# Attention's first head pair: raw q, k and bias rows loaded by ScalarE's queue, both heads in a row, k converted first

## The chip, the cores and the metric

The kernel runs on one core of a Trainium2 chip. The metric is the device time of one execution in microseconds. The kernel before takes a median of 1443.23 us over three runs (1440.9 to 1454.74). One profiled execution, from which all rows come, has a span of 1443.3 us from first to last instruction.

## The reference

One transformer block on a sequence of 1024 tokens and width 1024, all in float32. A vector `c` gives shifts, scales and gates; a normed and modulated `x` is projected by `w_in`. Half of the projection feeds eight heads of attention, the other half a gated delta rule. Both results go through `w_out`, and a gated feed-forward follows. The part that the change touches is attention:

```python
q_a, k_a, v_a, q_d, k_d, v_d, z_d, b_d, a_d = jnp.split(proj, split_points, axis=-1)
y_attn = _dilated_attention(q_a..., k_a..., v_a..., rel_bias)
# three branches (window, dilation) = (128, 1), (512, 4), (2048, 16), each:
s = jnp.einsum('bhrnqd,bhrnkd->bhrnqk', qb * dh ** -0.5, kw) + bias
m = jnp.max(s); e = jnp.exp(s - m); o = e @ v / sum(e)
# and the branches are mixed by a softmax over their log-sums
```

The kernel computes the three branches as one: every pair of positions gets one bias value per head, which holds the bucket's bias and the logarithm of the number of branches that see the pair, or minus 1e30 where none does.

## The kernel before

**Numbers.** A float32 operand of a matmul is split in a high part in the format fp32r and a low part (the rest after rounding), and two or three matmuls are summed. A conversion is therefore two instructions: a copy of ScalarE into the high tile, and a subtraction on GpSimd or VectorE for the low tile. In attention each head has 64 rows of q and 64 of k. A raw tile holds these 64 rows twice, in the upper and the lower 64 partitions, so it takes two loads of 64 rows and 256 KB each. `QS` holds q times -0.125, in one half of the partitions the high part and in the other the low part: ScalarE writes all of it (line 1223) and VectorE then overwrites one half with the rest (1224). `KS` is the high part of k (ScalarE, 1228) and `KL` its low part (GpSimd, 1229). A score is the matmul of `QS` with `KS` (1254) plus that with `KL` (1255). VectorE adds the bias from the tile `ng` while it leaves PSUM (1258); `ng` is 512 KB per head, read with a shifted row for each partition (1231). ScalarE takes the exponential (1263), GpSimd scales it (1265), TensorE turns it (1278) and multiplies it with the values `va` (1295).

**Stages.** After the first projections the delta rule runs, and its scan ends at about 477 us of the span. Then attention runs over four pairs of heads with eight query blocks each. `att_load` (1207) fetches a pair. Its data have been written to DRAM long before by `spill` (1071): for the first pair the last such write left at 430 us. Independent projections fill TensorE's gaps all along: `proj_t` (line 593) and `proj_d` (line 570) are generators whose matmuls are interleaved by `ahead`, `turn` and `attend`. Around the start of attention these are the values of the later pairs (`va1`, eight token blocks of 24 matmuls) and then k and q of the second pair (`a4_1`, `a0_1`). A finished block is copied from its PSUM bank by ScalarE (1061, 1070) and written to DRAM. There are two such banks (`gbank`, tag "g"), so a block can start only when the block before the last one has been copied out. The weights for them come in slabs (`wsplit`, 210): a load on SyncE's queue (215), a high part by ScalarE (216) and a low part by GpSimd (217); three raw, five high and five low slabs are in memory at once.

**Order.** A planner orders each engine's instructions: it walks through the program with estimated durations, and issues on each engine the instruction with the best priority among those that are ready in its walk. Priority is the place in the program; whatever stands in `with urgent():` is taken as 6000 places earlier. The order is fixed then: an engine that waits for one instruction holds back all that stands behind it. Before the change every DMA of the kernel is issued by SyncE (SP in the profile). The planner also gives each DMA one of eight completion counters in turn, shared by all queues, and an issue waits until the earlier DMA on its counter has landed. The tiles of attention (pool `pa`) lie in the memory of the delta rule's tiles (pool `pd`), which is closed just ahead; the four raw tiles lie on the tiles `qk` that the last readout of the scan reads (1011), and in the order of before the first load of the new pool stands behind the last write of the scan (1043).

Of the kernel before, what the change touches and what calls it, by code (L numbers as in the profile page):

```python
# [10 lines left out]
F32 = mybir.dt.float32  # L11
F32R = mybir.dt.float32r
AF = mybir.ActivationFunctionType
ALU = mybir.AluOpType
# [4 lines left out]
P = 128  # L19
T = 1024  # L20
# [50 lines left out]
def build(tc, I, out):  # L71
    nc = tc.nc
    es = ExitStack()
    op = es.enter_context

    def pool(name, side="left", bufs=1, space=None):
        st = ExitStack()
        kw = {} if space is None else {"space": space}
        p = st.enter_context(
            tc.tile_pool(name=name, bufs=bufs, side=side, reuse_waits="tile", **kw)  # L80
        )
        return p, st
# [10 lines left out]
    def urgent():  # L93
        return tc.high_priority(offset=6000)
# [10 lines left out]
        out=tri, in_=tri, pattern=[[1, P]], compare_op=ALU.is_ge, fill=0.0,  # L105
# [71 lines left out]
    for j in range(3):  # L177
        n = min(HALF, 1152 - HALF * j)
# [146 lines left out]
    for k in range(KT):  # L325
# [6 lines left out]
        if k == 0:  # L332
            for i in range(KT):
# [4 lines left out]
                out=G1[:, 0:1], in0=mod[:, 8:9], scalar=1.0, in1=ga[:, 0:1], op0=ALU.add, op1=ALU.mult  # L338
            )
            scaled(0, 1)  # L340
        for hf in range(2):
# [3 lines left out]
                out=hl[k][:, cs], in0=xts[k][:, cs], scalar=G1[:, k : k + 1], in1=hh[k][:, cs].bitcast(F32),  # L345
                op0=ALU.mult, op1=ALU.subtract,
# [160 lines left out]
    def scratch(name, n, shape):  # L507
        return [dr.tile(shape, F32, name=f"{name}{i}_d") for i in range(n)]

    class _:  # L510
        qk = scratch("qk", 8, [P, T])
        va = scratch("va", 2, [TB, P, 256])
# [42 lines left out]
    @contextmanager  # L555
    def turn(name):

        with tc.issue_after(last[0].ins) if ahead(FILL.get(name, 0)) else ExitStack():
            yield
# [75 lines left out]
    def v4(t):  # L635
        return t.rearrange("p (g n h) -> p g n h", g=2, n=8)
# [5 lines left out]
    for g in range(2):  # L642
        nc.vector.tensor_tensor(
            out=v4(t1)[:, g], in0=ba[:, 1, g], in1=dtb[:, 4 * g : 4 * g + 4].unsqueeze(1).to_broadcast([P, 8, 4]), op=ALU.add
# [553 lines left out]
    pa, sa = pool("pa")  # L1198
# [6 lines left out]
    yh, yl = {}, {}  # L1205

    def att_load(hp):
        va = pa.tile([P, TB, P], F32, name=f"va{hp}", tag="va", bufs=2)
        nc.sync.dma_start(va, _.va[hp // 2][:, :, P * (hp % 2) : P * (hp % 2) + P].rearrange("b p d -> p b d"))
        hs = []  # L1210
        for e in range(2):
            h = 2 * hp + e
            raws = []
            for kk in (0, 4):
                r = pa.tile([P, T], F32, name=f"raw{kk}_{h}", tag="raw", bufs=4)
                for i in range(2):
                    nc.sync.dma_start(r[64 * i : 64 * i + 64], _.qk[kk + hp][64 * e : 64 * e + 64, :])
                raws.append(r)
            QS = pa.tile([P, T], F32R, name=f"QS{h}", tag="QS", bufs=3)
            KS = pa.tile([P, T], F32R, name=f"KS{h}", tag="KS", bufs=3)  # L1220
            KL = pa.tile([P, T], F32R, name=f"KL{h}", tag="KL", bufs=3)
            low = slice(64 - 64 * e, 128 - 64 * e)
            nc.scalar.mul(QS, raws[0], -0.125)
            nc.vector.scalar_tensor_tensor(
                out=QS[low], in0=raws[0][low], scalar=-0.125, in1=QS[low].bitcast(F32),
                op0=ALU.mult, op1=ALU.subtract,
            )
            nc.scalar.copy(KS, raws[1])  # L1228
            nc.gpsimd.tensor_tensor(out=KL, in0=raws[1], in1=KS.bitcast(F32), op=ALU.subtract)
            ng = pa.tile([P, T], F32, name=f"ng{h}", tag="ng", bufs=2)  # L1230
            nc.sync.dma_start(
                ng,
                bass.AP(tensor=_.R.tensor, offset=_.R[h, 0:1, :].offset + 127, ap=[[1151, P], [1, T]]),
            )
            hs.append((QS, KS, KL, ng))
        return va, hs

    loaded = {}
    ybanks = {}
# [1 line left out]
    def att_score(hp, qb, e):  # L1241
# [3 lines left out]
        qs = slice(qb * P, qb * P + P)  # L1245
        QS, KS, KL, ng = loaded[hp][1][e]
        X = pa.tile([P, T], F32, name=f"X{h}_{qb}", tag="X", bufs=XB)
        sc = pa.tile([P, 4], F32, name=f"sc{h}_{qb}", tag="sc", bufs=6)
        m = None
        for c0 in range(0, nk, HALF):  # L1250
            c1 = min(nk, c0 + HALF)
            ps = scores(f"S{h}_{qb}_{c0}")
            with turn(f"S{h}_{qb}_{c0}"):
                nc.tensor.matmul(ps[:, 0 : c1 - c0], QS[:, qs], KS[:, c0:c1], start=True, stop=False)  # L1254
                nc.tensor.matmul(ps[:, 0 : c1 - c0], QS[:, qs], KL[:, c0:c1], start=False, stop=True)  # L1255
            i = c0 // HALF
# [53 lines left out]
    def attend(switch):  # L1310
        units = [(hp, qb) for hp in range(4) for qb in range(TB)]
        xs, ets = {}, {}
        for i in range(len(units) + AV):
            if i >= AV and units[i - AV] == (EARLY, 3):
                switch()
            if i < len(units):
                hp, qb = units[i]
                if hp not in loaded:
                    until(lambda: hp in done)
                    loaded[hp] = att_load(hp)  # L1320
                if i < EARLY * TB + 3 + AV:
                    ahead((FRONT - used[0]) / (EARLY * TB + 3 + AV - i))
                if qb >= 2 and hp < 3 and hp + 1 in done and hp + 1 not in loaded:
                    loaded[hp + 1] = att_load(hp + 1)
                xs[i] = [att_score(hp, qb, e) for e in range(2)]
            if AT <= i < len(units) + AT:
                hp, qb = units[i - AT]
                ets[i - AT] = [att_turn(hp, qb, e, xs[i - AT][e]) for e in range(2)]
                del xs[i - AT]
            if i >= AV:  # L1330
                hp, qb = units[i - AV]
                att_value(hp, qb, ets.pop(i - AV))
# [130 lines left out]
    for hf in range(2):  # L1463
# [4 lines left out]
        for d in range(KT):  # L1468
# [5 lines left out]
            with urgent():  # L1474
                nc.vector.scalar_tensor_tensor(
                    out=t, in0=ps, scalar=mod[:, 16 + d : 17 + d], in1=t, op0=ALU.mult, op1=ALU.add,
# [437 lines left out]
```

## Time and profile before

| | |
|---|---|
| median of three runs | 1443.23 us (1440.9 to 1454.74) |
| the profiled execution | 1445.04 us, its span 1443.3 us |
| granted TensorE clock, mean | 0.985 |
| TensorE busy | 1372.5 us, 95% of the span |
| VectorE, ScalarE, GpSimd busy | 61%, 46%, 21% |
| DMA, mean | 170 GB/s |
| the stretch 470 to 505 us | TensorE busy 23.94 of 35 us |

PE is TensorE, PEld its weight loads, DVE VectorE, ACT ScalarE, POOL GpSimd, SP SyncE; SPq is SyncE's queue, where a DMA_DIRECT2D row is the issue of a DMA and not its transfer. A row of a timeline gives start, duration, engine, line, operation and tiles (written <- read), and in brackets how long the engine was idle before it and what ended that. Matmuls overlap in the rows: their rate is read from the starts. "x4" at the end of a row means four instructions in one row.

### The profile page before, as it was taken

What the parts mean: (1) busy time and instruction counts of PE and PEld (TensorE: products, weight loads), DVE (VectorE), ACT (ScalarE), POOL (GpSimd) and SP (SyncE); (2) the same over time, 40 slices, a digit from 0 to 9 for tenths busy, and PEclk for the clock granted to TensorE, in tenths of its full rate; (3) what the DMA queues carried; (4) which work ended last, traced back from release to release, by engine and by line L of the source; (5) the groups of instructions that cost most, each with busy time, mean ns of one, the idle gap of its engine ahead of it and who ended that gap; (6) DMA issues with size and microseconds to landing.
All of it is one profiled execution on the core that took longest, in us unless ns stands there. A gap on an engine that the chain in (4) does not pass through costs nothing.

```text
span 1443.3 us, 24528 instructions
## 1 busy us (share of the span) xinstructions
PE 1372.5 (95%) x8984; PEld 1112.9 (77%) x8984; DVE 875.8 (61%) x1660; ACT 668.3 (46%) x1283; POOL 310.3 (21%) x279
## 2 busy tenths in 40 slices
PE   7998989997999699999998989999999999999997
PEld 4776857787879677777876868888888888888885
DVE  3587762665746223376426997757576776474487
ACT  3487523348233345576337743333333333444456
POOL 1345412243333334454244300000000000000000
PEclk9998999999999999999999999999999999999999
DMA  8736464466541643651375445636354565766666
GB/s 300 244 119 172 139 197 148 148 183 185 156 121 45 190 109 103 187 147 67 127 229 163 147 137 177 204 108 211 124 182 144 163 217 183 265 213 202 194 222 234
DMA packets 171921, 245.69 MB, mean 170 GB/s; under 512 B 33078, under 2 KB 76391, under 8 KB 171800
## 3 DMA queue, kind: packets, MB, share of 16 engines
q1 hardware_dynamic: 171800, 244.12, 54.4%
q8 instruction: 71, 1.16, 0.4%
q14 instruction: 50, 0.41, 0.1%
HBM read 181.30 MB, written 67.48 MB: 172 GB/s over the span
## 4 chain that ended last, share of the span: by engine, by line
PE 58%; DVE 6%; DMA 4%; ACT 2%; issue 1%; POOL 1%; SPq 0%; DVEq 0%; ACTq 0%; POOLq 0%
PE wua L1536 8%; PE wga L1536 8%; PE X L1731 6%; PE g_a L570 5%; PE wuc L1536 4%; PE Z L1731 4%; PE wgc L1536 4%; PE wo L570 3%; PE y L1295 2%; PE Y L1731 2%; PE tr L1278 2%; PE wgb L1536 2%; PE wub L1536 2%; PE g_va L593 2%; PE S L1254 1%
## 5 line engine op out<-in xcount | busy, mean ns | idle before, releaser
L1526 DVE TENSOR_TENSOR wl_db<-wr_db,wh_db 128x512 fp32r<-128x512 f32 x77 | 53.2, 691 | 76.4 <-ACT wh_db L1525 76.2
L1525 ACT CAST wh_db<-wr_db 128x512 fp32r<-128x512 f32 x77 | 47.9, 622 | 98.7 <-PE X L1731 41.3
L1258 DVE CUSTOM_DVE_ANT_0 X<-S,ng 128x512 f32<-128x512 f32 (+3 forms) x64 | 36.7, 587 | 71.5 <-PE S L1255 58.4
L1263 ACT ACTIVATE X<-X,sc 128x128 f32<-128x128 f32 (+7 forms) x64 | 49.4, 773 | 42.0 <-DVE sc L1258 36.6
L1731 PE MATMUL X<-wl_db,wh_da 128*128 128x512 f32 x176 | 68.6, 390 | 0.2 <-DVE wl_db L1526 0.2
L1731 PE MATMUL X<-wh_db,wh_da 128*128 128x512 f32 x176 | 68.6, 390 | 0.0
L1731 PE MATMUL X<-wh_db,wl_da 128*128 128x512 f32 x176 | 68.5, 389 | 0.0
L1265 POOL TENSOR_SCALAR X<-X,sc 128x128 f32<-128x128 f32 (+7 forms) x64 | 49.9, 782 | 82.3 <-DVE sc L1264 80.8
L1526 DVE TENSOR_TENSOR wl_da<-wr_da,wh_da 128x512 fp32r<-128x512 f32 x77 | 52.7, 686 | 1.2 <-ACT wh_da L1525 1.2
L570 PE MATMUL g_a<-hh,wh_a 128*128 128x512 f32 x128 | 53.2, 416 | 0.0
L570 PE MATMUL wo<-yh,wh_wo 128*128 128x512 f32 x128 | 51.5, 404 | 1.0 <-DVE xo L1346 1.0
L570 PE MATMUL wo<-yl,wh_wo 128*128 128x512 f32 x128 | 50.5, 394 | 0.9 <-DVE yl L1357 0.9
L570 PE MATMUL g_a<-hl,wh_a 128*128 128x512 f32 x128 | 51.0, 398 | 0.0
L570 PE MATMUL g_a<-hh,wl_a 128*128 128x512 f32 x128 | 50.7, 396 | 0.0
L570 PE MATMUL wo<-yh,wl_wo 128*128 128x512 f32 x128 | 50.6, 396 | 0.0
L1525 ACT CAST wh_da<-wr_da 128x512 fp32r<-128x512 f32 x77 | 47.3, 616 | 5.8 <-PE wua L1536 5.8
L1525 ACT CAST wh_wg_s<-wg_s 128x512 fp32r<-128x512 f32 x33 | 20.5, 622 | 55.4 <-PE wuc L1536 23.5
L1278 PE MATMUL tr<-ident,X 128*128 128x128 f32 x288 | 43.3, 277 | 2.8 <-DVE et L1281 1.8
L1254 PE MATMUL S<-KS,QS 128*128 128x512 f32 (+3 forms) x96 | 35.7, 380 | 10.2 <-ACT KS L1228 8.0
L217 POOL TENSOR_TENSOR wl_wo<-wr_wo,wh_wo 128x512 fp32r<-128x512 f32 x24 | 33.1, 1382 | 56.9 <-ACT wh_wo L216 55.9
L1295 PE MATMUL y<-et,va 128*64 128x128 f32 x576 | 42.8, 279 | 0.0
L1278 PEld LDWEIGHTS tr<-ident,X 128*128 128x128 f32 x288 | 33.0, 140 | 11.9 <-issue 4.6
(545 smaller groups left out, 4366.5 us busy)
## 6 DMA issues: line engine op xcount, KB each, us to landing
wr_da<-ao_d SPq DMA_DIRECT2D x77, 256.0 KB, 3.3
wm<-in_wada SPq DMA_DIRECT2D x64, 256.0 KB, 3.7
wr_wu<-in_wu SPq DMA_DIRECT2D x50, 256.0 KB, 2.9
wr_wg<-in_wg SPq DMA_DIRECT2D x48, 256.0 KB, 3.0
ao_d<-a SPq DMA_DIRECT2D x44, 256.0 KB, 2.7
wr_wd<-in_wdn SPq DMA_DIRECT2D x44, 256.0 KB, 3.1
wr_db<-wt_d SPq DMA_DIRECT2D x44, 256.0 KB, 3.0
ao_d<-as SPq DMA_DIRECT2D x33, 256.0 KB, 2.0
```

What stands on the lines that cost most here:

```text
L217: (eng or nc.gpsimd).tensor_tensor(out=lo[:, :n], in0=raw[:, :n], in1=hi[:, :n].bitcast(F32), op=ALU.subtract)
L570: last[0] = nc.tensor.matmul(ps, a[:, w0], b[k0 + k4][:, cs], start=(i == 0), stop=(i == n - 1))
L1254: nc.tensor.matmul(ps[:, 0 : c1 - c0], QS[:, qs], KS[:, c0:c1], start=True, stop=False)
L1258: nc.vector.tensor_tensor_reduce(out=X[:, c0:c1], in0=ps[:, 0 : c1 - c0], in1=ng[:, u + c0 : u + c1], scale=1.0, scalar=(3e38 if m is None ...
L1263: nc.scalar.activation(X[:, 0:nk], X[:, 0:nk], AF.Exp, scale=-1.0, bias=m, accum_out=sc[:, 2:3])
L1265: nc.gpsimd.tensor_scalar(out=X[:, 0:nk], in0=X[:, 0:nk], scalar1=sc[:, 3:4], scalar2=0.0, op0=ALU.mult, op1=ALU.add)
L1278: nc.tensor.transpose(ps[:, (kb - c0) * P : (kb - c0 + 1) * P], X[:, kb * P : kb * P + P], ident)
L1295: nc.tensor.matmul(yps[64 * e : 64 * e + 64, yc], va[:, kb, 64 * e : 64 * e + 64], ets[e][:, kb, :], start=(kb == 0), stop=(kb == qb),)
L1525: nc.scalar.copy(hi, src)
L1526: (eng or nc.vector).tensor_tensor(out=lo, in0=src, in1=hi.bitcast(F32), op=ALU.subtract)
L1536: nc.tensor.matmul(ps, a[:, w0], b, start=(first and k == 0 and n_ == 0), stop=(k == 3 and n_ == 2), skip_group_check=True,)
L1731: nc.tensor.matmul(bank[b], a[:, ts_], w, start=(first and f == 0 and n_ == 0), stop=(f == NF - 1 and n_ == 2), skip_group_check=True,)
```

## The change

The four raw loads of each head and its `ng` load are taken out of the loop over the two heads and traced together, ahead of the load of `va` and of all conversions: for each head k twice, q twice, then `ng`. For the first pair (`hp == 0`) these ten are issued on ScalarE's queue, and in `urgent()`; for the other three pairs they stay on SyncE's queue and without `urgent()`. In the conversions, for all pairs, `KS` and `KL` come ahead of `QS`. Tiles, their numbers of buffers, and the arithmetic stay as they were.

```diff
     def att_load(hp):
+        issue = nc.sync if hp else nc.scalar
+
+        def two(name, n, dt=F32):
+            return [pa.tile([P, T], dt, name=f"{name}{2 * hp + e}", tag=name, bufs=n) for e in range(2)]
+
         va = pa.tile([P, TB, P], F32, name=f"va{hp}", tag="va", bufs=2)
+        raws = {e: [pa.tile([P, T], F32, name=f"raw{kk}_{2 * hp + e}", tag="raw", bufs=4) for kk in (0, 4)] for e in range(2)}
+        QS, KS, KL = (two(name, 3, F32R) for name in ("QS", "KS", "KL"))
+        ng = two("ng", 2)
+        with ExitStack() if hp else urgent():
+            for e in range(2):
+                for kk in (4, 0):
+                    for i in range(2):
+                        issue.dma_start(
+                            raws[e][kk == 4][64 * i : 64 * i + 64], _.qk[kk + hp][64 * e : 64 * e + 64, :]
+                        )
+                issue.dma_start(
+                    ng[e],
+                    bass.AP(tensor=_.R.tensor, offset=_.R[2 * hp + e, 0:1, :].offset + 127, ap=[[1151, P], [1, T]]),
+                )
         nc.sync.dma_start(va, _.va[hp // 2][:, :, P * (hp % 2) : P * (hp % 2) + P].rearrange("b p d -> p b d"))
-        hs = []
         for e in range(2):
-            h = 2 * hp + e
-            raws = []
-            for kk in (0, 4):
-                r = pa.tile([P, T], F32, name=f"raw{kk}_{h}", tag="raw", bufs=4)
-                for i in range(2):
-                    nc.sync.dma_start(r[64 * i : 64 * i + 64], _.qk[kk + hp][64 * e : 64 * e + 64, :])
-                raws.append(r)
-            QS = pa.tile([P, T], F32R, name=f"QS{h}", tag="QS", bufs=3)
-            KS = pa.tile([P, T], F32R, name=f"KS{h}", tag="KS", bufs=3)
-            KL = pa.tile([P, T], F32R, name=f"KL{h}", tag="KL", bufs=3)
+            q, k = raws[e]
             low = slice(64 - 64 * e, 128 - 64 * e)
-            nc.scalar.mul(QS, raws[0], -0.125)
+            nc.scalar.copy(KS[e], k)
+            nc.gpsimd.tensor_tensor(out=KL[e], in0=k, in1=KS[e].bitcast(F32), op=ALU.subtract)
+            nc.scalar.mul(QS[e], q, -0.125)
             nc.vector.scalar_tensor_tensor(
-                out=QS[low], in0=raws[0][low], scalar=-0.125, in1=QS[low].bitcast(F32),
-                op0=ALU.mult, op1=ALU.subtract,
-            )
-            nc.scalar.copy(KS, raws[1])
-            nc.gpsimd.tensor_tensor(out=KL, in0=raws[1], in1=KS.bitcast(F32), op=ALU.subtract)
-            ng = pa.tile([P, T], F32, name=f"ng{h}", tag="ng", bufs=2)
-            nc.sync.dma_start(
-                ng,
-                bass.AP(tensor=_.R.tensor, offset=_.R[h, 0:1, :].offset + 127, ap=[[1151, P], [1, T]]),
-            )
-            hs.append((QS, KS, KL, ng))
-        return va, hs
+                out=QS[e][low], in0=q[low], scalar=-0.125, in1=QS[e][low].bitcast(F32), op0=ALU.mult, op1=ALU.subtract,
+            )
+        return va, list(zip(QS, KS, KL, ng))
```

## The prediction, made before the changed kernel had run

> **What bounds the kernel now.** I read the busy times by stage first.
>
> ```profile
> 470.00:505.00 35.00, 23.94 (x170) 21.94 (x169) 6.36 (x13) 12.13 (x23) 13.70 (x10) 0.90 0.65 192
> 505.00:560.00 55.00, 54.22 (x296) 42.83 (x295) 17.69 (x63) 27.93 (x64) 21.52 (x21) 0.97 0.39 105
> 560.00:613.00 53.00, 52.18 (x347) 41.88 (x346) 20.21 (x67) 27.68 (x64) 20.95 (x22) 1.00 0.56 160
> ```
>
> The columns are the stretch, its length, the busy time of PE, PEld, DVE, ACT and POOL, the granted clock, the DMA share and GB/s. From 505 to 613 us PE is busy for 106.4 of 108 us, so what starts earlier at 505 ends earlier. Just ahead PE loses 11 of 35 us. Where, the timeline of PE shows:
>
> ```profile
> 486.43 0.40 PE L570 MATMUL g_a<-hh,wh_a 128*128 128x512 f32 x1
> 486.67 0.40 PE L570 MATMUL g_a<-hl,wh_a 128*128 128x512 f32 x1
> ...
> 492.22 0.33 PE L1255 MATMUL S<-KL,QS 128*128 128x128 f32 x1 [1.39 <-POOL KL L1229]
> ...
> 502.15 0.80 PE L1254 MATMUL S<-KS,QS 128*128 128x128 f32 x2 [7.95 <-ACT KS L1228]
> 504.57 0.79 PE L1255 MATMUL S<-KL,QS 128*128 128x128 f32 x2 [1.63 <-POOL KL L1229]
> 505.17 0.63 PE L570 MATMUL g_a<-hh,wh_a 128*128 128x512 f32 x1
> ...
> 508.47 0.40 PE L570 MATMUL g_a<-hh,wl_a 128*128 128x512 f32 x1
> ```
>
> PE waits 1.39 us for the first head's `KL` and 7.95 + 1.63 for the second's `KS` and `KL`. The eight steps from 505.17 to 508.47 take 3.30 us; at the spacing of 486.43 to 486.67 (0.24) they take 1.9. So 1.4 more goes to a low clock. **Removable: 1.39 + 7.95 + 1.63 + 1.4 = 12.4 us.** The second head is late because of SyncE's queue:
>
> ```profile
> 478.39 0.32 SPq L1062 DMA_DIRECT2D va_d<-va  x1
> 478.81 0.39 SPq L1209 DMA_DIRECT2D va<-va_d  x1
> 479.25 2.53 SPq L1217 DMA_DIRECT2D raw<-qk_d  x4
> 486.38 3.82 SPq L215 DMA_DIRECT2D wr_a<-in_wd  x3
> 490.25 0.42 SPq L1231 DMA_DIRECT2D ng<-Rb_d  x1
> 490.77 0.45 SPq L1217 DMA_DIRECT2D raw<-qk_d  x1
> ...
> 493.81 1.73 SPq L1217 DMA_DIRECT2D raw<-qk_d  x3
> ```
>
> The queue's own waits there, with total, times and longest:
>
> ```profile
> SPq L215 <- POOL wl_a L217: 9.3, 4, 4.5
> ```
>
> After the first head's four raw issues the queue takes slab loads, which wait for a free slab. Behind them stand the first `ng` and the second head's raw loads; the last three leave from 493.81, 12 us after the first head's last.
>
> **The change part by part.** *Loads out of SyncE's queue.* Ten issues no longer stand behind the slab waits. Their memory is free and their data written by then, so they can leave once ScalarE reaches them. This makes the 12.4 us removable; what it brings is what the next waits leave of it. The slab loads themselves wait for POOL as before, and `va`, now traced behind the ten, stays on SyncE; its first reader, by the chain of waits, comes only at
>
> ```profile
> 523.49 0.37 PE y L1295 x4
> ```
>
> so nothing on SyncE gets worse.
>
> *Loads into ScalarE's queue.* The planner put the first load of the new pool behind the scan's last write; I take the same place here, behind ScalarE's copy at 477.99. As `urgent()` and earlier in the program, all ten precede the block copies that follow:
>
> ```profile
> 477.99 0.37 ACT L1061 COPY va<-g_va 128x256 f32<-128x256 f32 x1 [1.13 <-PE g_va L593]
> 480.92 0.37 ACT L1061 COPY va<-g_va 128x256 f32<-128x256 f32 x1 [2.55 <-PE g_va L593]
> 483.80 0.37 ACT L1061 COPY va<-g_va 128x256 f32<-128x256 f32 x1 [2.51 <-PE g_va L593]
> ...
> 485.60 1.05 ACT L1223 ACTIVATE QS<-raw 128x1024 fp32r<-128x1024 f32 x1
> ```
>
> No row of this kernel shows ScalarE issuing a DMA. The nearest are SyncE's issues of the same loads (ns, least, median and most), the queue's waits at that line, the landing of the third load alone, and the two `ng` issues:
>
> ```profile
> L1217 SPq DMA_DIRECT2D raw<-qk_d x32: 444/588/657, 479.2 to 625.4; - x32
> L1217 SPq EVENT_SEMAPHORE  x10: 17/17/2191, 480.6 to 623.6; - x10
> ...
> DMA to landing us min/median/max: 5.8/5.8/5.8
> ...
> L1231 SPq DMA_DIRECT2D ng<-Rb_d x2: 425/504/583, 490.2 to 495.6; - x2
> ```
>
> The third of the first four raw loads landed 5.8 us after its issue. Ten issues take 8 x 0.588 + 2 x 0.504 = 5.7 us, from 478.4 to 484.1. But there are eight completion counters, and `va` (on SyncE, meanwhile) takes one or two; so the last three or four loads wait for the first to land: the first at 478.4 + 0.6 + 5.8 = 484.8, then one per 0.6. ScalarE is free at about **486.3** (484.1 if no counter holds it).
>
> Behind it stand the copies of the blocks that end at 480.9 and 483.8, then slab copies and the conversions. PE has two banks: the last `va1` block (483.7 on) needs the bank of the block that ended at 480.9. Its copy is done at 486.3 + 0.4 = 486.7. **PE waits 3.0 us** (bounds 0.8, if ScalarE is free at 484.1, and 22.9, worked out in the last rival).
>
> Whether this wait costs clock too:
>
> ```profile
> 488.00:492.00 4.00, 2.83 (x13) 2.00 (x12) 0.69 (x1) 2.35 (x3) 4.00 (x2) 1.00 0.58 189
> 492.00:496.00 4.00, 1.98 (x9) 1.54 (x9) 0.46 (x3) 0.49 (x2) 1.75 (x3) 1.00 0.86 301
> 496.00:500.00 4.00, 0.00 (x0) 0.00 (x0) 1.22 (x1) 1.06 (x1) 0.02 (x1) 0.76 0.94 235
> 500.00:504.00 4.00, 0.80 (x2) 0.50 (x2) 0.00 (x0) 1.75 (x3) 1.82 (x1) 0.50 0.84 274
> ```
>
> The idle 1.39 us at 491 left the clock at 1.00; 7.95 us brought it to 0.50. By these rows alone a 3.0 us wait costs 0 to 1.4; nearer to 1.39, I take 0. The Trainium skill, page "TensorE: Matmul & The Clock Gate", Part 1, puts the halving after an idle window of about 3.4 us: with it too the sum stays, and a wait half a microsecond longer would lose the 1.4; no row here shows a wait between.
>
> *The conversions, k first.* These rows carry the next steps:
>
> ```profile
> 485.05 4.79 POOL L217 TENSOR_TENSOR wl_a<-wr_a,wh_a 128x512 fp32r<-128x512 f32 x3 [10.11 <-PE g_va L593]
> 489.81 2.36 POOL L1229 TENSOR_TENSOR KL<-raw,KS 128x1024 fp32r<-128x1024 f32 x1
> ...
> L1223 ACT ACTIVATE QS<-raw x8: 1042/1056/1062, 485.6 to 651.8; 128x1024 fp32r<-128x1024 f32 x8
> ...
> L1224 DVE SCALAR_TENSOR_TENSOR QS<-raw,QS x8: 1218/1612/2935, 486.7 to 653.2; 64x1024 fp32r<-64x1024 f32 x8
> ```
>
> First head: two block copies to 487.1, `KS` to 488.1, `QS` to 489.2, VectorE's half to 490.4 to 491.2. PE ends the `va1` block at 486.7 + 2.9 = 489.6. If the score comes at once it waits up to 1.6, if behind 15 matmuls as before nothing: **0.8**. `KL` comes ahead of the three slab halves (done 490.5) or behind them (485.05 + 3.0 + 4.8 + 2.4 = 495.2): 0 to 1.4, as the wait of before: **0.7**. Second head: PE reaches it after 24 matmuls of 0.23, at about 497. The eight raw loads (2 MB), two `ng` (1 MB) and `va` (0.5) make 3.7 MB; at the 274 GB/s of 500 to 504 they take 13.5 us, so k lies at about 489, q at 491, `ng` at 492, and `KL` ends by 497.6 even behind slabs and first head: **0.3**. In later pairs `QS` comes one instruction (1.05) later for VectorE and `KL` one earlier for POOL; PE's scores need both. Six heads at most 1.05 each way, 6 us. Who waited for VectorE's half over the whole run:
>
> ```profile
>   PE S L1254: 1.5, 1
> ```
>
> PE, once, for 1.5 us; so I take 0.
>
> **Sum:** 12.4 - 3.0 - 0.8 - 0.7 - 0.3 = **7.6 us less**, 1445.04 to 1437.4 in the profiled execution's own time (span 1443.3). That execution lies 1.8 above the median of 1443.23, so I forecast 1443.2 - 7.6 = **1435.6**. The low end is 12.4 - 0.8 = 11.6 less and another 3 from the later pairs.
>
> **The rivals.** *All land together (1441.6).* If the ten loads share the engines evenly, the first head's k lands with the last, at 492 rather than 485. Then `KS`, `QS` and VectorE's half end at 495.9 and PE waits 6.3 us at 489.6, and loses the clock's 1.4: 12.4 - 3.0 - 7.7 = 1.7 less. For it: 235 to 301 GB/s is all that moved while raw loads were open. Against: the first head's four raw loads were used from 485.60 on, though all were issued by 481.8 with `va` ahead. The Trainium skill, page "DMA: Bandwidth & Descriptors", "Issuing engines are not separate DMA queues", speaks against the change in the same way: all issuers share 16 DMA engines, and another queue saves only issue time. That agrees with the cap in those rows.
>
> *The loads go further up (1440.2).* The raw tiles' last readers end at 472:
>
> ```profile
> 472.07 0.37 ACT L1016 COPY o<-o 128x256 f32<-128x256 f32 x1 [0.85 <-PE o L1011]
> 476.00 0.41 PE L1038 MATMUL yt<-ident,o 128*128 128x128 f32 x2
> ```
>
> If the planner sees them free there, the ten issues stand ahead of this copy, from 472 to about 480. The chain from the copy to the turn at 476.00 takes 3.9, so PE stops from 476 to 483.9 and loses the clock: 7.9 + 1.4 = 9.3, leaving 3.0 less. Against it: the first loads of before came behind the scan's last write.
>
> *ScalarE is held at each issue (1456.7), the slower side.* If each issue waits as the longest did on SyncE (2.191 + 0.588), ten take 27.8 us and ScalarE is free at 506.2. PE idles from 483.7 to 506.6, 22.9, plus 1.4 of clock and 1.6 for the first head: 25.9 against 12.4, so 13.5 more. It decides at 1.4 us per issue, where ScalarE is free at 492.6. Against: the median wait there is 17 ns.
>
> **How the numbers follow.** Forecast (4 to 12 less): 0.60. All together (1 more to 4 less): 0.14. Further up: 0.07. Held at each issue, or a replanned later stage that costs more than is won: 0.11. More than 12 less (no counter wait, later pairs gain): 0.08. The range leaves out most of the last two: **1428 to 1446**. A measurement of this kernel can tell about 1% from no change, here 14.4 us, so below 1428.8 or above 1457.6. Faster by that: 0.05, most of the last case; slower by it: 0.05 of the 0.11, as that rival's own time is just inside; within: 0.90.
>
> **What would show it.** Ten DMA issues in one run on ScalarE behind the copy of 478, lasting some 8 us; the next block copy late, and PE idle some 3 us at 483.7 with the clock still at 1.00; raw loads gone from SyncE ahead of 490; the wait of 7.95 for `KS` gone and the first score of the second head at about 497 in place of 502. Wrong would be: issues spread between ScalarE's copies (no PE wait, more gain), a wait for `KS` or VectorE's half over 3 us, or PE idle in 505 to 700 where it was busy.

## The result, and the profile after

The changed kernel takes **1450.91 us** at the median of 20 runs (1446.63 to 1457.58) against 1445.32 us (1440.9 to 1454.74, 20 runs) for the kernel before on the same chip: a ratio of **1.0035, 95% interval 1.002 to 1.0051**, so 3 to 7 us slower. The forecast was 7.6 us less. The profiled execution has a span of 1446.2 us. All ratios here are taken over the executions at the usual clock; the few that ran at a lower one are left out.

The first two of the stretches in the prediction, in the changed kernel (length, busy time of PE, PEld, DVE, ACT and POOL, granted clock, DMA share, GB/s):

```profile
470.00:505.00 35.00, 22.07 (x151) 20.91 (x149) 7.40 (x13) 8.95 (x18) 10.05 (x7) 0.80 0.66 167
505.00:560.00 55.00, 52.87 (x282) 42.58 (x283) 15.37 (x59) 27.47 (x65) 23.92 (x24) 1.00 0.44 117
```

PE is busy for 22.07 us of the first 35, where it was 23.94: the idle time that was to go is still there, and 1.4 us has been added behind 505. The timeline of PE shows that it has moved. These are the rows with a wait of over 1 us between 483 and 510:

```profile
496.33 0.58 PE L593 MATMUL g_va<-wh_va,hh 128*128 128x256 f32 x1 [12.48 <-ACT va L1061]
505.75 0.30 PE L1256 MATMUL S<-KS,QS 128*128 128x128 f32 x1 [1.09 <-DVE QS L1235]
```

The waits for `KS` and `KL` (1.39, 7.95 and 1.63 before) are gone. In their place PE stands for 12.48 us ahead of the last `va1` block, until ScalarE has copied an earlier block out of its bank. The timeline of ScalarE tells why (ACTq rows are DMA issues):

```profile
478.13 0.37 ACT L1061 COPY va<-g_va 128x256 f32<-128x256 f32 x1 [1.14 <-PE g_va L593]
478.14 2.44 ACTq L1221 DMA_DIRECT2D raw<-qk_d  x4
480.61 0.66 ACTq L1224 DMA_DIRECT2D ng<-Rb_d  x1
482.35 5.54 ACTq L1221 DMA_DIRECT2D raw<-qk_d  x4
495.48 0.33 ACTq L1224 DMA_DIRECT2D ng<-Rb_d  x1
495.90 0.65 ACT L1061 COPY va<-g_va 128x256 f32<-128x256 f32 x2 [17.40 <-DMA va<-va_d]
```

Ten issues stand in one run behind the copy of 478, as forecast. Nine have left by 487.9. The tenth, the second head's `ng`, leaves at 495.48, and the two block copies behind it only then. SyncE's queue and the landing of its second `va` load show what it waited for:

```profile
478.90 1.39 SPq L1228 DMA_DIRECT2D va<-va_d  x2
```

```profile
L1228 SPq DMA_DIRECT2D va<-va_d x1: 793/793/793, 479.5 to 479.5; - x1
...
DMA to landing us min/median/max: 16.0/16.0/16.0
```

The second of the two is the *second* pair's `va`. The kernel before issued it behind everything else:

```profile
497.16 0.47 SPq L1209 DMA_DIRECT2D va<-va_d  x1
```

With the raw loads gone from SyncE's queue the planner issues it at 479.5, beside the row. It landed 16.0 us later, at 495.5, and the tenth issue left at 495.48. In the built order the two share a completion counter: of the eight, given out in turn, the tenth issue on ScalarE gets the one of that load. So ScalarE waited for a DMA that none of its own work needs.

The clock, in stretches of 4 us of the changed kernel, and one of the kernel before, which follows on the last that the prediction shows:

```profile
484.00:488.00 4.00, 0.00 (x0) 0.00 (x0) 0.00 (x0) 0.00 (x0) 0.00 (x0) 1.00 1.16 241
488.00:492.00 4.00, 0.00 (x0) 0.00 (x0) 0.00 (x0) 0.00 (x0) 0.00 (x0) 0.59 1.07 284
492.00:496.00 4.00, 0.00 (x0) 0.00 (x0) 0.00 (x0) 0.10 (x1) 0.00 (x0) 0.50 0.50 114
496.00:500.00 4.00, 3.67 (x17) 3.67 (x18) 1.52 (x1) 4.00 (x7) 2.43 (x2) 0.50 0.68 197
500.00:504.00 4.00, 4.00 (x19) 3.68 (x19) 2.08 (x4) 2.31 (x4) 4.00 (x2) 0.70 0.22 25
```

```profile
504.00:508.00 4.00, 3.42 (x9) 2.85 (x10) 1.40 (x9) 1.74 (x7) 1.85 (x4) 0.50 0.10 33
```

In the changed kernel PE works at half clock from 496.3 to about 502.4 us, 6.0 us without a gap. In the kernel before it does from 502.2 to about 508.3, but the wait of 1.63 us lies in that, so it is 4.6 us of work. If work takes twice as long at half clock, the low clock cost about 3.0 us after and 2.3 before (an estimate from these rows). The rest is idle time: the waits of over 0.25 us in the 100 us behind the scan sum to 15.5 us after and 12.2 before. The stage as a whole can be read from two rows of PE in each kernel, the scan's last turn and the first matmul of the output projection, before (its `yt` row, at 476.00, stands in the prediction) and after:

```profile
613.08 0.39 PE L570 MATMUL wo<-yh,wh_wo 128*128 128x512 f32 x1
```

```profile
476.13 0.41 PE L1038 MATMUL yt<-ident,o 128*128 128x128 f32 x2
...
616.68 0.39 PE L570 MATMUL wo<-yh,wh_wo 128*128 128x512 f32 x1
```

From the second of the two `yt` matmuls (0.14 behind the row's start) it takes 136.9 us before and **140.4 after: 3.5 us more**, which lies in the interval of the measured times. I call this time the *attention stretch*; it is free of what happens ahead of the scan's end, which differs by up to 6 us between profiled executions. Each value of it comes from one execution; how much it varies between executions of one kernel was not measured, so some tenths of a microsecond in it prove nothing alone.

### The profile page after: what moved, and what is told of

Its sections match the earlier page's. It is cut to its first block, busy times and chain, and to the rows that moved or that the text cites. A ratio compares the mean times of both kernels' runs of the same rounds, so it can differ in the third digit from the quotient of the medians.

```text
span 1446.2 us, 24523 instructions
## 1 busy us (share of the span) xinstructions
PE 1375.5 (95%) x8984; PEld 1117.0 (77%) x8984; DVE 878.0 (61%) x1660; ACT 667.4 (46%) x1283; POOL 311.2 (22%) x279
## 4 chain that ended last, share of the span: by engine, by line
PE 58%; DVE 5%; DMA 4%; issue 2%; ACT 1%; POOL 0%; SPq 0%; ACTq 0%; DVEq 0%; POOLq 0%
PE wua L1538 8%; PE wga L1538 8%; PE X L1733 6%; PE g_a L570 4%; PE wuc L1538 4%; PE wgc L1538 4%; PE Z L1733 4%; PE wo L570 3%; PE y L1297 2%; PE Y L1733 2%; PE tr L1280 2%; PE wgb L1538 2%; PE wub L1538 2%; PE g_va L593 1%; PE S L1256 1%
## 5 line engine op out<-in xcount | busy, mean ns | idle before, releaser
L593 PE MATMUL g_va<-wh_va,hh 128*128 128x256 f32 x128 | 39.5, 309 | 12.6 <-ACT va L1061 12.5
```

Of the source, the lines that this page charges most:

```text
L593: last[0] = nc.tensor.matmul(ps[:, :n], a[k][:, ts_], b[:, w0], start=(i == 0), stop=(i == 23))
```

## The experiments

Theory: ScalarE is held at an issue by the counter of a load that has not landed, and PE behind it by the block copies. The rivals: the issues themselves hold ScalarE; the conversions' new order costs; the loads land late whoever issues them. The code cuts are shortened; "..." stands for what is left out.

### The bias rows on SyncE's queue

```diff
-                issue.dma_start(
+                nc.sync.dma_start(
                     ng[e],
```

> The changed kernel with the two bias loads of the first pair on SyncE's queue (still urgent); the eight raw loads stay on ScalarE's. Theory A (the tenth issue, the second head's bias load, waits for the counter that the second pair's va load holds, and that load took 16.0 us beside the row, so ScalarE is held to 495.5): no raw load stands behind that counter now, ScalarE is free at about 488 as after its ninth issue before, PE waits about 4.5 us in place of 12.5, and the time is 3 to 8 us under the kernel before. Theory B (any row on ScalarE's queue costs what it gains, since block copies stand behind it): 0 to 5 us over the kernel before, as the change.

Measured: 1446.83 us, ratio 0.9992 (0.9971 to 1.0013); attention stretch 136.9 us.

```profile
480.44 11.89 ACTq L1221 DMA_DIRECT2D raw<-qk_d  x8
492.45 0.65 ACT L1061 COPY va<-g_va 128x256 f32<-128x256 f32 x2 [11.64 <-DMA raw<-qk_d]
...
492.88 0.58 PE L593 MATMUL g_va<-wh_va,hh 128*128 128x256 f32 x1 [6.72 <-ACT va L1061]
```

Two issues fewer on ScalarE bring the loss back to nothing, but the eight that are left still hold it for 11.9 us, where eight times 0.6 would be 4.8. The expectation had ScalarE free at 488 and 3 to 8 us won; neither came. The eighth raw issue waits here for the counter of the second bias load, as the kernel with the same loads further down shows.

### The second pair's `va` held back

The load is tied to the first pair's last spill, so that it leaves at 527 us; the ten stay on ScalarE.

```diff
...
-        nc.sync.dma_start(va, ...)
+        with tc.issue_after(spilled[0].ins) if hp == 1 else ExitStack():
+            nc.sync.dma_start(va, ...)
```

> The changed kernel, but the second pair's va load may leave only behind the last write of the second pair's q, so it is not in flight beside the row; all ten loads stay on ScalarE's queue. Theory A: the tenth issue then waits for a raw load of the first head only, ScalarE is free at 487 to 488, PE waits 4 to 5 us, 3 to 8 us under the kernel before. Theory B: 0 to 5 us over it. A third one (the ten loads are bound by the transfers and land as late as 495 anyhow): ScalarE is free early, but PE waits for the second head's KS or QS until 497 or later, within 2 us of the kernel before.

Measured: 1450.2 us, ratio 1.0016 (0.9993 to 1.004); attention stretch 135.4 us, 5 less than in the changed kernel.

```profile
488.80 0.60 ACTq L1226 DMA_DIRECT2D ng<-Rb_d  x1
489.50 0.65 ACT L1061 COPY va<-g_va 128x256 f32<-128x256 f32 x2 [10.11 <-DMA ng<-Rb_d]
...
489.92 0.58 PE L593 MATMUL g_va<-wh_va,hh 128*128 128x256 f32 x1 [5.19 <-ACT va L1061]
```

The tenth issue now follows the ninth at once, and PE's wait falls from 12.48 to 5.19 us. That is the kernel that the prediction had in mind, with 5.19 for its 3.0. The 5 us show in the stretch alone; in the measured time, 1.0 us less to 5.8 more than before, no gain is shown, where 3 to 8 us were expected.

### The whole row on SyncE's queue

```diff
-        issue = nc.sync if hp else nc.scalar
+        issue = nc.sync
```

> The changed kernel with the row of ten on SyncE's queue, urgent, ScalarE issuing nothing. Theory A and B alike: no block copy is held, PE does not wait at the last va1 block; the slab loads stand behind the row to about 488, which PE needs only from the second half of the next block on. 6 to 10 us under the kernel before. If the row itself (its order and its ten transfers at once) were what costs, it would be as slow as the change, 3 to 6 us over the kernel before.

Measured: 1446.74 us, ratio 0.998 (0.9961 to 0.9999); attention stretch 136.5 us. PE does not wait at the `va1` block at all. But two waits are left, PE's here with VectorE's that makes the second:

```profile
500.47 0.45 PE L1256 MATMUL S<-KS,QS 128*128 128x128 f32 x1 [2.94 <-DVE QS L1235]
...
541.07 0.58 PE L1256 MATMUL S<-KS,QS 128*128 128x256 f32 x1 [2.34 <-DVE sc L1260]
```

```profile
537.97 1.06 ACT L1234 ACTIVATE QS<-raw 128x1024 fp32r<-128x1024 f32 x1 [2.15 <-DMA raw<-qk_d]
539.06 1.22 DVE L1235 SCALAR_TENSOR_TENSOR QS<-raw,QS 64x1024 fp32r<-64x1024 f32 x1 [6.79 <-ACT QS L1234]
```

VectorE stands 6.79 us ahead of the second pair's `QS` half, which k first has put last, and the first pair's scores wait to be evacuated behind it. In the kernel before VectorE waited 4.76 us there, and PE 0.31. A gain of 6 to 10 us was expected; the ratio gives 0.1 to 5.7. The low clock behind the two waits took most of it, as the last section shows.

### k first alone

The kernel before, all on SyncE, head by head, with k loaded and converted first.

```diff
-            for kk in (0, 4):
+            for kk in (4, 0):
...
+            k, q = raws
+            nc.scalar.copy(KS, k)
+            nc.gpsimd.tensor_tensor(out=KL, in0=k, in1=KS.bitcast(F32), op=ALU.subtract)
             nc.scalar.mul(QS, q, -0.125)
```

> The kernel before with k ahead of q in the loads and in the conversions, nothing else: all loads on SyncE's queue, head by head. By every theory here within 2 us of the kernel before, as the second head's loads stay behind the slab loads; if k first is what costs in the later pairs, 3 to 6 us over it.

Measured: 1450.63 us, ratio 1.0007 (0.9981 to 1.0033); attention stretch 140.0 us, 3.1 more than before.

```profile
505.77 0.45 PE L1255 MATMUL S<-KS,QS 128*128 128x128 f32 x1 [12.36 <-DVE QS L1227]
```

The three waits of before (10.97 us) become one of 12.36 at the second head, for VectorE's half of `QS`. k first gains nothing: the score needs `QS` as well, and it comes last instead. The time, 2.8 us less to 4.8 more than before, decides between neither of the two expectations.

### The row on SyncE's queue, the later pairs as before: q first, and k first

`att_load` of the kernel before serves pairs 1 to 3. The first of the two kernels loads and converts the first pair's q first, the second k.

```diff
     def att_load(hp):
+        if hp:
+            return att_load_old(hp)
-        issue = nc.sync if hp else nc.scalar
+        issue = nc.sync
```

> Of the kernel before only one thing changes: the first pair's ten loads go out in a row on SyncE's queue, ahead of the first va load and the weight rows. q is converted first, as before, and pairs 1 to 3 are as before. Theory A (the row itself is worth something, k first costs in the later pairs): the 7.95 us wait goes, about 3 us of waits at the first scores stay, no new score wait near 61 to 67 us behind the scan's last matmul (0.31 us in before, 1.2 to 2.3 us in every kernel with k first in all pairs), and the time is 3 to 5 us under before. Theory B (the row earns nothing, since what comes behind it absorbs it): within 1.5 us of before. By the order of the first pair alone, q first: the first score needs QS, VectorE's half, KS and GpSimd's KL, the same four, so I expect it within 0.5 us of the next kernel.

> The row on SyncE's queue with k converted first in the first pair only; pairs 1 to 3 as before. Against the row on SyncE's queue with k first in all pairs (2.34 us of score wait 60.7 us behind the scan's last matmul): theory A, that the wait comes from the second pair's q conversions standing last, says the wait falls to 0.3 to 0.5 us and the time is 1.5 to 3 us lower than there, 3 to 5 us under before. Theory B, that the wait belongs to the first pair's own pace (whatever arrives early there waits later), says that a wait of about 2 us stays at that place.

Measured: q first 1444.6 us, ratio 0.9986 (0.9965 to 1.0007), attention stretch 132.1 us, 4.9 under before; k first 1441.76 us, ratio 0.9986 (0.9963 to 1.0009). No row of the second is shown, so only its time counts here.

```profile
492.26 0.47 PE L1290 MATMUL S<-KL,QS 128*128 128x128 f32 x1 [3.12 <-POOL KL L1270]
503.11 0.50 PE L570 MATMUL g_a<-hh,wh_a 128*128 128x512 f32 x1 [1.91 <-ACT va L1061]
```

In the first, the wait behind the second pair's conversions is 0.39 us where it was 2.34 with k first in all pairs; q first in the first pair differs as well, so the next kernel has to show which of the two does it. In the measured times neither kernel differs from the row with k first everywhere; the 3 to 5 us that I expected stand in the first kernel's stretch and not in a ratio.

### The changed kernel, the later pairs as before

> The changed kernel with pairs 1 to 3 taken back to the kernel before: q first, head by head. Theory A: the tenth issue still holds ScalarE to about 495 us and PE idles about 12.5 us at the second va block, since the planner's place for the second pair's va load is the same; the score wait of 1.17 us at 67 us falls to 0.3 us, and the time is 1 to 2 us under the changed kernel, still 1 to 3 us over before. Rival: the later pairs' order is the whole loss, and the time comes out at or under before.

Measured: 1450.13 us, ratio 1.0027 (1.0005 to 1.005); attention stretch 139.8 us.

```profile
497.93 0.33 ACTq L1257 DMA_DIRECT2D ng<-Rb_d  x1
...
498.77 0.58 PE L593 MATMUL g_va<-wh_va,hh 128*128 128x256 f32 x1 [12.87 <-ACT va L1061]
```

The wait at the `va1` block is there again, 12.87 us, and so is the loss. The 1.17 us behind the second pair's conversions are gone with the first pair unchanged, so that wait does come from the later pairs' order; it costs 0.6 us of the stretch, if that difference of two single executions is not scatter. The rival that it is the whole loss falls.

### Eight on ScalarE, the bias rows on SyncE, the later pairs as before

The edit of the first kernel, and that of the kernel just above.

> The eight raw loads in a row on ScalarE's queue, the two bias loads on SyncE's, pairs 1 to 3 as before: both suspected costs taken away at once, the counter wait in part. With the bias rows on SyncE and k first everywhere, PE idled 6.72 us at the second va block, 1.82 and 1.84 us at scores, and the time was level with before. Theory A: the 1.84 us falls to 0.3, and the time is 1 to 3 us under before; SyncE's row stays ahead of it by the 6 us that PE waits at the va block less the wait for scores there, 2 to 4 us. If it is level with SyncE's row, ScalarE's hold is not what matters.

Measured: 1446.46 us, ratio 1.0003 (0.9986 to 1.0019); attention stretch 136.1 us. In the timeline PE waits 6.70 us at the `va1` block. The groups of the raw line and of the bias line give the counter a second time:

```profile
L1254 ACTq DMA_DIRECT2D raw<-qk_d x8: 452/548/628, 479.7 to 491.1; - x8
...
L1257 SPq DMA_DIRECT2D ng<-Rb_d x2: 494/552/611, 480.4 to 481.0; - x2
...
DMA to landing us min/median/max: 10.1/10.1/10.1
```

In the built order the eighth raw issue has the counter of the second bias load. That left SyncE at 481.0 and landed 10.1 us later, at 491.1; the eighth raw issue left at 491.1. One issue takes 0.55 us, so ScalarE was not held by issuing. The wait behind the second pair's conversions is 0.46 us as expected; the 1 to 3 us are not in the time.

### Six loads on ScalarE, and six on SyncE

Each raw tile is filled by one load that reads its 64 rows twice. Pairs 1 to 3 are as in the kernel before, and on SyncE's queue q comes first.

```diff
-                    for i in range(2):
-                        issue.dma_start(raws[e][kk == 4][64 * i : 64 * i + 64], _.qk[kk + hp][64 * e : 64 * e + 64, :])
+                    src = _.qk[kk + hp][64 * e : 64 * e + 64, :]
+                    issue.dma_start(raws[e][kk == 4], bass.AP(tensor=src.tensor, offset=src.offset, ap=[[0, 2], *src.ap]))
```

> The row stays on ScalarE's queue, but each raw tile is filled by one load that reads its 64 rows twice instead of two loads of 64 rows, so the row is six issues and not ten; pairs 1 to 3 as before. Six issues need six of the eight completion counters, so in the built order no issue of the row waits for a load of the row, nor for a va load; the last one waits for the write of the va1_4 block alone. Theory A (ScalarE is held by counters): ScalarE is through the row at 4.5 to 6 us behind its start instead of 17.7 (ten issues), PE's wait at the second va block falls from 12.9 us to 0 to 1.5 us although the second va load is still issued beside the row, and the time is 2 to 5 us under before. Theory B (the loads on ScalarE's ring land late whatever the counters, 7 to 9 us): the conversions of k and q wait instead, PE waits 4 us or more at the first scores, and the time is level with before. Theory C (the issues themselves hold ScalarE): six of them at twice the size take as long as ten, 8 us or more.

> The same six loads in a row on SyncE's queue, q first, pairs 1 to 3 as before. With ten loads on SyncE's queue PE waited 3.12 us at the first score and 1.91 us for weight rows behind it. Theory A (SyncE's row is limited by its issues, 0.6 us each, and by counters): the row ends 2 to 4 us earlier, the 1.91 us goes, the 3.12 us falls to 1 to 2.5 us, and the time is 3 to 6 us under before. Theory B (it is limited by the 3 MB that must land): the same waits, and a time within 1 us of the ten loads' kernel.

Measured: 1478.09 us, ratio 1.0219 (1.019 to 1.0249), and 1473.15 us, ratio 1.0187 (1.0158 to 1.0216). None of the theories had such a loss in it. With the row on ScalarE, PE's wait, two of ScalarE's issues, and a stretch in which no engine works and only the row and `va` loads can still be open:

```profile
516.77 0.58 PE L593 MATMUL g_va<-wh_va,hh 128*128 128x256 f32 x1 [29.88 <-ACT va L1061]
```

```profile
482.85 10.17 ACTq L1257 DMA_DIRECT2D ng<-Rb_d  x1
...
506.19 10.06 ACTq L1257 DMA_DIRECT2D ng<-Rb_d  x1
```

```profile
500.00:516.00 16.00, 0.00 (x0) 0.00 (x0) 0.00 (x0) 0.00 (x0) 0.00 (x0) 0.50 0.13 52
```

52 GB/s move, at a share of 0.13 of the 16 DMA engines, which is two of them; at that rate 512 KB take 10 us. With the row on SyncE it is 54 GB/s at the same share from 488 to 500 us.

The Trainium skill, page "DMA: Bandwidth & Descriptors", "Rules for kernel authors", says so: the outermost dimension of a transfer sets over how many engines it spreads, and a leading repeat of two copies confines it to at most two. These rows agree. So the pair of runs was an error in the experiment and says nothing on six issues against ten. One thing it does show: an issue can itself be long. The two above last 10 us, where the same loads took 0.66 and 0.33 us to issue in the changed kernel; why is not shown.

### Ten on ScalarE, the second pair's `va` held back, the later pairs as before

The edits of the second kernel and of the changed kernel with the later pairs as before, together.

> The ten loads on ScalarE's queue, the second pair's va load held back until the first pair's last spill write, pairs 1 to 3 otherwise as before: both of the causes that I hold for the loss are taken out of the changed kernel. With the va load held back alone PE waited 5.19 us at the second va block and 1.61 us at a score, and 1.86 us at a score 60.9 us behind the scan's last matmul. Theory A: the first two stay (the counters of the row's own first loads and of the first va load hold ScalarE to about 10 us behind its start), the third falls to 0.3 to 0.5 us, and the time is 1 to 4 us under before. Rival: the time stays at or over before, and the loss has another cause than these two.

Measured: 1443.09 us, ratio **0.9979 (0.9958 to 1.0000)**; attention stretch 135.1 us, 1.9 under before and 5.3 under the changed kernel.

```profile
486.62 0.58 PE L593 MATMUL g_va<-wh_va,hh 128*128 128x256 f32 x1 [4.57 <-ACT va L1061]
497.27 0.30 PE L1293 MATMUL S<-KS,QS 128*128 128x128 f32 x1 [3.06 <-DVE QS L1272]
```

With both causes out the change is no longer slower than before, while all ten issues are still ScalarE's; 1 to 4 us less were expected, and 0 to 6 are measured.

### Only the first head's four raw loads on ScalarE

The six other loads of the row are SyncE's, and pairs 1 to 3 are as in the kernel before.

```diff
-        issue = nc.sync if hp else nc.scalar
+        row = (nc.scalar, nc.sync)
...
-                        issue.dma_start(
+                        row[e].dma_start(
                             raws[e][kk == 4][64 * i : 64 * i + 64], _.qk[kk + hp][64 * e : 64 * e + 64, :]
                         )
-                issue.dma_start(
+                nc.sync.dma_start(
                     ng[e],
```

> Only the first head's four raw loads go out on ScalarE's queue; the two bias loads and the second head's four raw loads go out on SyncE's, in the row's order; pairs 1 to 3 as before. In the built order the four issues on ScalarE share no counter with a load that is still under way, so by theory A (ScalarE is held by counters of loads under way) ScalarE is through them 2.4 to 3 us behind their start, against 17.7 for ten and 11.9 for eight, PE waits 0 to 0.5 us at the second va block against 12.9 and 6.7, the wait is at the scores instead (2 to 6 us in all, as with the whole row on SyncE's queue), and the time is 1 to 4 us under before. Theory B (DMA issues on ScalarE cost PE by themselves, one by one, whatever the counters): PE still waits 2 us or more at the second va block, half of what eight issues cost.

Measured: **1438.59 us, ratio 0.9952 (0.9932 to 0.9972)**; attention stretch 129.4 us, 7.6 under before. ScalarE's, SyncE's and PE's timelines:

```profile
479.61 2.44 ACTq L1254 DMA_DIRECT2D raw<-qk_d  x4
482.52 0.37 ACT L1061 COPY va<-g_va 128x256 f32<-128x256 f32 x1 [2.55 <-PE g_va L593]
...
480.37 1.16 SPq L1257 DMA_DIRECT2D ng<-Rb_d  x2
481.57 0.58 SPq L1261 DMA_DIRECT2D va<-va_d  x1
483.63 3.71 SPq L1254 DMA_DIRECT2D raw<-qk_d  x4
...
492.92 0.30 PE L1289 MATMUL S<-KS,QS 128*128 128x128 f32 x1 [2.43 <-DVE QS L1268]
499.90 0.50 PE L570 MATMUL g_a<-hh,wh_a 128*128 128x512 f32 x1 [1.49 <-ACT va L1061]
```

Four issues take 2.44 us and none waits: the next copy starts when PE has its block ready, and the wait at the `va1` block is gone. Counter waits still occur, but on SyncE (its row begins at 483.63), where they cost less: the second head's raw loads stand behind them, and ScalarE waits 3.69 us for one of these at 495.05, ahead of the block copy that PE waits 1.49 us for. This version beats both kernels, and by more than the 1 to 4 us expected: 4 to 10 us under before.

Side by side (PE's waits of 0.25 us and more, in us, summed in each place; "second" is the wait behind the second pair's conversions, "-" is none):

| kernel | ratio to before | attention stretch | `va1` block | first pair's scores | second |
|---|---|---|---|---|---|
| before | 1 | 136.9 | - | 10.97 | 0.31 |
| changed | 1.0035 | 140.4 | 12.48 | 1.09 | 1.17 |
| bias on SyncE | 0.9992 | 136.9 | 6.72 | 1.82 | 1.84 |
| `va` held back | 1.0016 | 135.4 | 5.19 | 1.61 | 1.86 |
| row on SyncE | 0.998 | 136.5 | - | 3.46 | 2.34 |
| k first alone | 1.0007 | 140.0 | - | 12.36 | 1.90 |
| row on SyncE, q first, later as before | 0.9986 | 132.1 | - | 3.12 | 0.39 |
| changed, later as before | 1.0027 | 139.8 | 12.87 | 1.53 | - |
| eight, bias on SyncE, later as before | 1.0003 | 136.1 | 6.70 | 2.06 | 0.46 |
| ten, `va` held back, later as before | 0.9979 | 135.1 | 4.57 | 3.06 | 0.84 |
| four on ScalarE, later as before | 0.9952 | 129.4 | - | 2.43 | - |

## Why the prediction was wrong

**The place and the mechanism of the new wait were right, its length was not.** The prediction had the ten issues behind the copy of 478, ScalarE held by counters, the copies of two blocks behind them and PE waiting for the bank at the last `va1` block. It gave that 3.0 us, with bounds of 0.8 and 22.9; it measured 12.48. The step that failed is "ScalarE is free at about 486.3"; it was free at 495.9. Three things in that step were wrong:

- It looked for the counters' earlier users among the row's own loads. Nine issues were through at 487.9, where it had all ten through at 486.3, but not for that reason. ScalarE was held at three issues, and in the built order each of them has the counter of a DMA of SyncE's: the sixth (1.1 us) that of a block's write, the eighth (3.3 us) that of the first `va` load, the tenth (7.6 us) that of the second. The prediction counted "`va` (on SyncE, meanwhile)" as taking one or two counters and went on as if these came free early.
- It took "nothing on SyncE gets worse" as the whole of what happens to SyncE's queue. A queue that is emptied is filled with what stood behind: the second pair's `va` moved from 497.16 to 479.5, ahead of the issue that then had to wait for it.
- It gave every load the 5.8 us of one raw load. In the changed kernel the raw loads on ScalarE's queue whose landing the view gives took 7.2 to 9.2 us, and the second `va` load 16.0.

The rival "held at each issue" had the right end, slower, and named ScalarE; it put the price on every issue. Seven of the ten were not held, and three were, for 12 us in all. Its point of decision, ScalarE free at 492.6, was a good one: 495.9 lies past it, and the kernel is slower. The two rivals near 1441 did not happen: the issues stand where they were forecast, and the conversions did not wait for the loads to land together, since they stood behind ScalarE's hold anyway. (Their sums give 1441.5 and 3.1 where the prediction has 1441.6 and 3.0; nothing hangs on it.)

**The clock.** The prediction had 1.4 us of low clock to win, from eight steps behind 505.17, and 0 to lose. The low clock of before spans the scores at 502 as well and costs about 2.3 us, so the term was undersized; and a wait of 12.48 us brought it back, at about 3.0 us. Nothing was won, and 0.7 lost. The Trainium skill, page "TensorE: Matmul & The Clock Gate", Part 1, has the clock halve after an idle window of about 3.4 us; the trace agrees in so far as 12.48 us is past it and the granted clock is 0.50 when PE resumes. It asks for too much, though, as the last section shows.

**The first scores.** 0.8 + 0.7 + 0.3 = 1.8 us were expected, 1.09 measured. The first score of the second head came at 505.75, not at 497, since all behind ScalarE's hold had moved.

**The later pairs.** They were set to 0, with up to 3 us of gain at the low end. They lost: PE waits 1.17 us for evacuations behind the second pair's `QS` half. Taking the later pairs back shortened the stretch by 0.6, 0.8 and 0.3 us in three pairs of kernels, each from single executions. The argument, that in the kernel before PE waited for VectorE's half only once, holds only for the order of before.

**The sum** with the measured terms: idle time of over 0.25 us 15.5 for 12.2, low clock 3.0 for 2.3, so 4.0 more, where the stretch shows 3.5. Freeing the tenth issue would not have saved the forecast: in the kernel with `va` held back PE still waits 5.19 us, the half clock behind that wait and behind one of 1.86 us later costs about 4 us, and the stretch is 1.5 us under before, not 7.6. That the waits of before can be removed was rightly read: the version with four issues on ScalarE takes 7.6 us out of the stretch. That this is just the size forecast for ten is chance, since that forecast had taken off 3.0 us for a wait at the bank which this version does not have, and had counted on no low clock, where this version has 3.4 us of it.

Left open: why the `va` load took 16.0 us. Beside raw loads on ScalarE's queue `va` loads took 11.5 to 16.4 us in five kernels, behind a row on their own queue 4.6 and 6.3. A `va` load has rows of 512 bytes and a raw load rows of 4 KB, but no run changed the size of the rows alone.

## What to carry to other kernels

An engine that computes and also issues DMAs is held by whatever load has the completion counter that its issue is given, also by loads of other queues that it has no use for: follow each issue to the earlier user of its counter, and take that load's landing time, not the issue time. When loads leave a queue, ask what the planner puts in their place and when, for it will fly beside them. Keep the issues on a compute engine few, under the number of counters less what other queues have in flight, and put those for which something waits soonest there, the rest on the idle queue.

## What was not expected of the hardware

**A load spread by its outermost dimension.** A source with a leading repeat of two moved at 52 to 54 GB/s, where loads over 128 or 64 rows reached 241 to 284 GB/s in the changed kernel's rows.

**Half clock behind waits under 3.4 us.** In the kernel with four issues on ScalarE, PE's only wait over 1.5 us there is the 2.43 us that end at 492.92. Directly behind it:

```profile
488.00:492.00 4.00, 2.49 (x12) 1.73 (x10) 0.61 (x1) 1.34 (x2) 4.00 (x4) 1.00 1.08 293
492.00:496.00 4.00, 3.08 (x9) 2.54 (x10) 1.07 (x3) 0.95 (x1) 1.91 (x1) 0.64 1.03 231
```

In the kernel with the row on SyncE, behind the wait of 2.34 us that ends at 541.07:

```profile
540.00:544.00 4.00, 2.93 (x10) 1.99 (x11) 2.70 (x10) 1.48 (x4) 0.00 (x0) 0.57 0.56 138
544.00:548.00 4.00, 4.00 (x15) 3.27 (x14) 0.42 (x3) 2.05 (x5) 1.94 (x3) 0.57 0.00 0
```

Read in stretches of half a microsecond, the half clock lasts 3.4 us in the first (493.1 to 496.5) and 6.8 in the second (540.6 to 547.4). In the kernel with the row on SyncE there is another one of 10.2 us, from 499.6, behind the wait of 2.94 us. By the work done in them the two cost that kernel about 7.6 us (an estimate) where the kernel before lost 2.3. These 5.3 us more are as much as it won by waiting 7.1 us in place of 12.2. So a wait under 3.4 us can cost clock, where the prediction took a wait of 3.0 us to be free. The Trainium skill, page "TensorE: Matmul & The Clock Gate", Part 1, asks for an idle window of about 3.4 us; the rows decide.

The length of the wait does not settle it either. Waits of 1.78 us (eight on ScalarE, ending at 501.5), 1.82 us (bias on SyncE, 502.3) and 1.86 us (`va` held back, 538.0) were each followed by 3.4 us of half clock. Waits of 1.84 us (bias on SyncE, 542.5), 1.90 us (k first alone, 543.8) and 1.91 us (row on SyncE with q first, 503.1) left it at 1.00, as did 1.39 us (before, at 491) and 1.17 us (changed kernel, second pair). The periods of half clock here are one, two, three or four times 3.4 us long; in steps of that length, counted from a change of the clock in the same trace, each of the first three waits lies inside one step and each of the next three across two. That this decides was not tested.
